# Layer 1's low weight parts made by an accumulating DMA instead of a subtraction on DVE

## The chip, the cores and the metric

The kernel runs on one core of one Trainium2 chip, as one program with one launch. The metric is the device time of an execution in microseconds (us). An execution that was recorded by the hardware profiler gives the rows that are read here; a profiled execution's span runs from its first to its last instruction.

## The reference, cut to what matters

A trunk of two layers over 512 positions with 1024 channels, in float32, then a final norm:

- Layer 0 is a hybrid of two recurrent mixers (an S5 state space and a Mamba-2 SSD), with an input projection, gates and an output projection.
- Layer 1 is multi-scale retention: RMSNorm, one input projection [q | k | v | gate] with 4 heads (256 wide for q and k, 512 wide for v), rotary on q and k, the decayed scores and their product with v, a norm per head, `silu(gate)` times the normed output, an output projection, and the residual add.

```python
p = (h @ w_in).astype(F32)                 # 1024 x 6144
...
y = jax.nn.silu(g) * o
return y.astype(w_out.dtype) @ w_out       # 2048 x 1024
```

The kernel computes its weight products with float32r matmuls. It writes each operand as a high part (the value as rounded to float32r) and a low part (what is left of it), and sums three products: high by high, high by low, low by high.

## The kernel before, in words

Activations stand transposed, channels on partitions and the 512 positions along the free axis; each 128-channel piece has a high tile and a low tile made once. Weights come from HBM as tiles of 128 x 8 x 128 numbers (512 KB). `ld_w` (L93) takes a raw buffer (tag `raw`, two of them), has SP start the load (L96) and calls `split_w` (L99), which takes a high buffer (tag `wh`, two) and a low buffer (tag `wl`, two) and issues two instructions: ACT copies raw into the float32r high tile, which rounds it (L105), and DVE subtracts the high tile from raw into the low tile (L106). `mm3` (L109) then runs 24 matmuls of 128x128 by 128x512 per tile, three for each of the 8 k: high weight by high activation (L113), high weight by low activation (L114), low weight by high activation (L115), all into one PSUM bank. So a tile's low part is first read by its third matmul.

Layer 1 takes 60 tiles through `ld_w`: for each head 4 for q and k (named `qk...`, by `proj`, L848) and 4 for v (`v...`, L882, with 4 PSUM banks at a time, L887 to L889), 16 for the gate (`g0` to `g15`, L943), 8 for the first half of the output projection (`out0` to `out7`, L960) and 4 for the second half's first columns (`on0` to `on3`, L993, L998 to L1000). The order in the program is qkv(0), qkv(1), gate(0), gate(1), out0 to out7, qkv(2), qkv(3), gate(2), gate(3), on. The second half's last columns (`om0` to `om3`, L1003 to L1011) load into the same `raw` buffers, but are split by `split` (L117), halves of 512 columns with ACT (L118) and DVE (L119), into buffers of their own. Everything else that PE does in layer 1 (scores and their products with v, L874; norms, L164 and L170; transposes, L971) goes between the tiles' matmuls.

POOL does little in layer 1: the rotary's sums (`rt`, L861), the sums of squares of a head's output (`os`, L930) and of the layer's input (`hs`, L840), and one product of the final norm (L1023).

No order is written by hand here. The builder (a tile framework) tracks which instruction reads and writes which buffer, plays the program through a model of the engines' times, and puts each engine's instructions in the order in which they become ready there, ties by rank: `rank_w` (L86) gives weight splits a rank ahead of all else after the setup, `rank_e` (L90) gives evictions the next. On the chip each engine then takes its instructions strictly in that order, each waiting on semaphores for what it needs. A buffer is taken again when the last reader of its former tile is done: `wh` after the last L114 of the tile two before, `wl` after its last L115, `raw` after its split.

Of the kernel before, what the change touches and what calls it, by code (L numbers as in the profile page):

```python
# [11 lines left out]
F32 = mybir.dt.float32  # L12
F32R = mybir.dt.float32r
I32 = mybir.dt.int32
AF = mybir.ActivationFunctionType
ALU = mybir.AluOpType

P = 128
SEQ = 512
D = 1024  # L20
KD = D // P
# [27 lines left out]
def trunk_kernel(ctx: ExitStack, tc: tile.TileContext, a: dict, out: bass.AP):  # L49
    nc = tc.nc  # L50
    vec, act, pool, pe, sp = nc.vector, nc.scalar, nc.gpsimd, nc.tensor, nc.sync

    cp = ctx.enter_context(tc.tile_pool(name="cp", bufs=1))
    wp = ctx.enter_context(tc.tile_pool(name="wp", bufs=2))
# [16 lines left out]
        return t  # L71

    wcount = [0]
    wdma = {}

    def after(name):
# [2 lines left out]
    @contextmanager  # L79
    def rank(v):  # L80
        old = tc.cur_priority
        tc.cur_priority = v
        yield
        tc.cur_priority = old

    def rank_w():  # L86
        wcount[0] += 1
        return rank(-2000000 + 20 * wcount[0])
# [4 lines left out]
    def ld_w(src, name, halves=1, ahead=0):  # L93
        raw = wp.tile([P, KD, P], F32, name=name + "w", tag="raw", bufs=2)
        with rank(tc.cur_priority - ahead):
            wdma[name] = sp.dma_start(raw, src).ins  # L96
        return split_w(raw, name, halves)

    def split_w(raw, name, halves=1):  # L99
        h = wp.tile([P, KD, P], F32R, name=name + "h", tag="wh", bufs=2)  # L100
        lo = wp.tile([P, KD, P], F32R, name=name + "l", tag="wl", bufs=2)
        n = KD // halves
        with rank_w():
            for k in range(0, KD, n):
                act.activation(h[:, k:k + n], raw[:, k:k + n], AF.Copy)  # L105
                vec.tensor_tensor(lo[:, k:k + n], raw[:, k:k + n], h[:, k:k + n].bitcast(F32), op=ALU.subtract)  # L106
        return h, lo
# [77 lines left out]
    def layer0():  # L185
        xh, xl, sq = [], [], []

        def proj(src, name, tag="acc", ahead=0):
            ps = acc(name) if tag == "acc" else aux(name, tag)
            mm3(ps, ld_w(src, name, ahead=ahead), xh, xl)  # L190
            return ps
# [268 lines left out]
        for m in range(8):  # L460
            ps = acc(f"gl{m}")
            mm3(ps, ld_w(a["w_glu"][m], f"gl{m}"), y5h, y5l)
            with rank_e():
                sg = t("p", f"sg{m}")
                act.activation(sg, ps, AF.Sigmoid, bias=chp[:, 3, m:m + 1])
                vec.tensor_tensor(sg, sg, za[m], op=ALU.mult)
                h, lo = t("x", f"yah{m}", F32R), t("x", f"yal{m}", F32R)
                split(sg, h, lo)
            yah.append(h), yal.append(lo)
        for m in range(KD):  # L470
            ps = acc(f"ob{m}")
            mm3(ps, ld_w(a["w_o0"][m, 1], f"ob{m}"), ybh, ybl)
            with rank_e():
                if m % 2 == 0:
                    xp = f(f"h{m}", [P, 2, SEQ])
                x = xp[:, m % 2]
                with after(f"ob{m}"):
                    sp.dma_start(x, a["xT"][m])
                vec.tensor_tensor(x, ps, x, op=ALU.add)  # L479
                hT.append(x)  # L480
# [546 lines left out]
                sp.dma_start(out[c * P:(c + 1) * P, i * 512:(i + 1) * 512], fin[c][i])  # L1027

    layer0()
    layer1()  # L1030


# [60 lines left out]
def _build(arrays):  # L1093
    import concourse.bacc as bacc

    nc = bacc.Bacc("TRN2", target_bir_lowering=False, num_devices=1)
    aps = {k: nc.dram_tensor(f"in_{k}_dram", v.shape, F32, kind="ExternalInput").ap() for k, v in arrays.items()}
    out = nc.dram_tensor("out_0_dram", (SEQ, D), F32, kind="ExternalOutput").ap()
    with tile.TileContext(nc, schedule_with_timeline_sim=True) as tc:
        trunk_kernel(tc, aps, out)  # L1100
    return nc
# [9 lines left out]
```

## Time and profile before

| what | value |
|---|---|
| time, three executions | 935.73, 935.9, 938.51 us; median 935.9 |
| profiled execution, span | 934.4 us (the page lists no other time of this execution) |
| PE (matmul) busy | 857.8 us, 92% of the span |
| DVE busy | 637.8 us, 68% |
| ACT busy | 350.3 us, 37% |
| POOL busy | 287.0 us, 31% |
| moved by DMA | 117.47 MB |

PE is TensorE's matmuls (PEld its weight loads, which overlap them), DVE is VectorE, ACT ScalarE, POOL GpSimd, SP the engine whose queue issues the DMAs. Shares of busy time are averages over stages with different limits: layer 0 fills the first 500 us or so, layer 1 the rest, and DVE's 68% is mostly layer 0's. In a timeline row the bracket says how long the engine was idle before the instruction and what ended that idle time.

### The profile page before, as it was taken

How to read it: one execution, taken by the hardware profiler on the slowest of the kernel's cores; microseconds unless marked ns; L12 is line 12 of the kernel's file. 1: busy time of each engine (PE TensorE's matmuls, PEld its weight loads, DVE VectorE, ACT ScalarE, POOL GpSimd, SP SyncE). 2: the span in 40 equal slices, each digit the busy share in tenths (PEclk: the TensorE clock that was granted, in tenths of full speed). 3: DMA queues.
4: the chain of work that ended last, by engine and by line, in shares of the span. 5: the costliest groups of instructions: out<-in, count | busy, mean ns of one | idle time of the engine just before them, and what ended most of it. 6: DMA issues, size and time to landing. Idle time of an engine off the chain costs nothing.

```text
span 934.4 us, 11848 instructions
## 1 busy us (share of the span) xinstructions
PE 857.8 (92%) x4408; PEld 691.0 (74%) x4408; DVE 637.8 (68%) x1086; ACT 350.3 (37%) x504; POOL 287.0 (31%) x217
## 2 busy tenths in 40 slices
PE   7995589788888988899999999999999999999996
PEld 5773467666666876677888888888888888888885
DVE  7999999999999468885344454744633644447455
ACT  5132124111235677564233235245421243254432
POOL 7039963576755223900013021201000303110020
PEclk9997789978899999899999999999999999999999
DMA  5376357545478876224423221221223221212322
GB/s 168 113 186 164 73 143 198 158 120 167 136 191 271 257 240 237 80 101 147 180 90 107 94 85 54 90 71 66 90 93 109 90 83 54 90 68 67 113 91 90
DMA packets 71609, 117.47 MB, mean 126 GB/s; under 512 B 27328, under 2 KB 37888, under 8 KB 71424
## 3 DMA queue, kind: packets, MB, share of 16 engines
q1 hardware_dynamic: 71552, 116.72, 40.4%
q8 instruction: 35, 0.57, 0.3%
q14 instruction: 22, 0.18, 0.1%
HBM read 101.71 MB, written 14.97 MB: 125 GB/s over the span
## 4 chain that ended last, share of the span: by engine, by line
PE 57%; DVE 1%; ACT 0%; issue 0%; ACTq 0%
PE g L113 3%; PE qk L115 3%; PE qk L114 3%; PE g L115 3%; PE g L114 3%; PE qk L113 3%; PE v L889 3%; PE v L887 3%; PE v L888 3%; PE ob L113 2%; PE oa L114 2%; PE oa L115 2%; PE oa L113 2%; PE ob L114 2%; PE ob L115 2%; PE out L115 1%
## 5 line engine op out<-in xcount | busy, mean ns | idle before, releaser
L861 POOL TENSOR_TENSOR rt<-rt,ru 128x512 f32<-128x512 f32 x16 | 27.2, 1721 | 137.6 <-DVE ru L860 137.6
L930 POOL TENSOR_TENSOR os<-os,os 128x512 f32<-128x512 f32 x12 | 15.5, 1291 | 143.3 <-ACT os L928 143.3
L840 POOL TENSOR_TENSOR hs<-hs,hs 128x512 f32<-128x512 f32 x7 | 12.6, 1805 | 105.0 <-ACT hs L838 105.0
L325 DVE SCALAR_TENSOR_TENSOR cva<-pad,cvw,cva 128x512 f32<-128x512 f32 x36 | 40.9, 1140 | 0.1
L860 DVE TENSOR_TENSOR ru<-qk,tab 128x512 f32<-128x512 f32 x16 | 10.9, 683 | 33.7 <-PE qk L115 33.7
L762 POOL TENSOR_TENSOR O<-ct,s5pws 128x512 f32<-128x512 f32 x16 | 22.8, 1427 | 32.4 <-DMA ct<-in_s5c_dram 20.6
L327 ACT ACTIVATE cva<-cva 128x512 f32<-128x512 f32 x12 | 7.6, 630 | 55.2 <-DVE cva L325 55.2
L323 ACT ACTIVATE cva<-pad,cvw 128x512 f32<-128x512 f32 x12 | 9.8, 813 | 49.2 <-DVE pad L321 49.2
L766 POOL TENSOR_TENSOR O<-O,ot 128x512 f32<-128x512 f32 x16 | 27.6, 1747 | 0.1
L762 POOL TENSOR_TENSOR ot<-ct,s5pws 128x512 f32<-128x512 f32 x16 | 26.6, 1661 | 0.6 <-DVE mg L746 0.6
L377 POOL TENSOR_TENSOR ssdb<-ssdb,cva 128x1024 f32<-128x1024 f32 x6 | 17.4, 2905 | 29.9 <-ACT ssdb L376 23.5
L1023 POOL TENSOR_TENSOR fin<-fin,fnw 128x512 f32<-128x512 f32 x4 | 6.0, 1525 | 61.5 <-ACT fq L987 61.5
L962 DVE TENSOR_TENSOR h<-h,out 128x512 f32<-128x512 f32 x8 | 5.5, 686 | 25.5 <-PE out L115 25.5
L479 DVE TENSOR_TENSOR h<-ob,h 128x512 f32<-128x512 f32 x8 | 5.5, 690 | 25.4 <-PE ob L115 25.4
L486 DVE TENSOR_TENSOR h<-h,oa 128x512 f32<-128x512 f32 x8 | 5.5, 688 | 21.9 <-PE oa L115 21.9
L366 DVE TENSOR_SCALAR ssdb<-ssdb,nacs 128x128 f32<-128x128 f32 x64 | 15.2, 303 | 6.8 <-DMA ssdb<-at_d 6.8
L712 POOL TENSOR_TENSOR tm<-al,b 128x512 f32<-128x512 f32 x6 | 10.4, 1750 | 29.2 <-DMA b<-in_s5bP_dram 22.8
L383 PE MATMUL y<-ssdb,xdt 128*64 128x128 f32 x128 | 13.8, 300 | 4.6 <-DVE ssdb L368 4.6
L371 POOL TENSOR_TENSOR xds<-xdt,dcd 128x512 f32<-128x512 f32 x6 | 7.6, 1270 | 32.1 <-DVE xdt L356 32.1
L491 POOL TENSOR_TENSOR s5rt<-rot,s5lv 128x512 f32<-128x512 f32 (+4 forms) x7 | 5.6, 803 | 38.1 <-DVE s5lv L647 35.8
L367 ACT ACTIVATE ssdb<-ssdb 128x1024 f32<-128x1024 f32 x8 | 8.5, 1057 | 23.1 <-DVE ssdb L366 23.1
L383 PEld LDWEIGHTS y<-ssdb,xdt 128*64 128x64 f32 x128 | 9.0, 145 | 9.9 <-DVE ssdb L368 5.3
(1784 smaller groups left out, 3177.2 us busy)
## 6 DMA issues: line engine op xcount, KB each, us to landing
al<-al_d SPq DMA_DIRECT2D x64, 64.0 KB, 3.5
b<-in_s5bP_dram SPq DMA_DIRECT2D x8, 512.0 KB, 4.2
o_d<-O SPq DMA_DIRECT2D x16, 256.0 KB, 2.7
T<-kd SPq DMA_DIRECT2D x64, 64.0 KB, 3.6
ssdb<-at_d SPq DMA_DIRECT2D x8, 512.0 KB, 4.9
Or<-o_d SPq DMA_DIRECT2D x16, 256.0 KB, 4.8
x<-in_xT_dram SPq DMA_DIRECT2D x8, 256.0 KB, 5.0
u_d<-us SPq DMA_DIRECT2D x8, 256.0 KB, 3.1
```

The costliest lines, as they stand in the source:

```text
L113: pe.matmul(ps, wh[:, k, :], xh[k], start=start and i == 0, stop=False)
L114: pe.matmul(ps, wh[:, k, :], xl[k], start=False, stop=False)
L115: pe.matmul(ps, wl[:, k, :], xh[k], start=False, stop=stop and i == len(ks) - 1)
L325: vec.scalar_tensor_tensor(g, pad[:, j:j + SEQ], cvw[:, m, j:j + 1], g, op0=ALU.mult, op1=ALU.add)
L377: pool.tensor_tensor(abc, abc, cT[gr][:, cs].unsqueeze(1).broadcast_to([P, 8, P]), op=ALU.mult)
L383: pe.matmul(o, xdt[:, i, :], dec[:, i, :], start=True, stop=c == 0)
L762: pool.tensor_tensor(x.rearrange("p (g k c) -> p g k c", g=4, c=16), ct[:, c, par, 4 * hf:4 * hf + 4].unsqueeze(2).broadcast_to(sh), pws[: ...
L766: pool.tensor_tensor(o, o, tm, op=ALU.add)
L861: pool.tensor_tensor(t1, t1, t2, op=op)
L887: pe.matmul(ps[c], hh[kk][:, cs], wh[:, i, :], start=kk == 0, stop=False)
L888: pe.matmul(ps[c], hh[kk][:, cs], wl[:, i, :], start=False, stop=False)
L889: pe.matmul(ps[c], hl[kk][:, cs], wh[:, i, :], start=False, stop=kk == KD - 1)
```

## The change

In layer 1 (a flag is set between the two layers) `ld_w` splits a tile with a new function. ACT makes the high part as before, then a second copy of raw with scale -1 into the low buffer, again as float32r, which is the negative of the high part. POOL then issues a DMA that adds raw to the low buffer, both in SBUF, so that it holds raw minus the high part. DVE has no part in it. Layer 0 and the `om` tiles keep the subtraction.

```diff
     wcount = [0]
+    by_dma = [False]
     wdma = {}
...
-        return split_w(raw, name, halves)
+        return split_d(raw, name) if by_dma[0] else split_w(raw, name, halves)
+
+    def split_d(raw, name):
+        h = wp.tile([P, KD, P], F32R, name=name + "h", tag="wh", bufs=2)
+        lo = wp.tile([P, KD, P], F32R, name=name + "l", tag="wl", bufs=2)
+        with rank_w():
+            act.activation(h, raw, AF.Copy)
+            act.activation(lo, raw, AF.Copy, scale=-1.0)
+            pool.dma_start(lo.bitcast(F32), raw, accum_op=ALU.add)
+        return h, lo
...
     layer0()
+    by_dma[0] = True
     layer1()
```

## Rows read from the trace of the kernel before

**Rows 1.** The page's busy time of each engine.

```profile
PE 857.8 (92%) x4408; PEld 691.0 (74%) x4408; DVE 637.8 (68%) x1086; ACT 350.3 (37%) x504; POOL 287.0 (31%) x217
```

**Rows 2.** By stretch: busy us (count) of PE, PEld, DVE, ACT, POOL; clock; DMA.

```profile
514.70:602.00 87.30, 87.30 (x407) 71.98 (x406) 47.28 (x83) 31.15 (x48) 18.75 (x12) 1.00 0.23 79
...
858.00:903.40 45.40, 45.40 (x216) 37.38 (x215) 22.85 (x30) 19.81 (x31) 0.00 (x0) 1.00 0.34 116
...
sum 419.70, PE 411.34 PEld 339.52 DVE 214.78 ACT 155.63 POOL 50.45; mean PE 58.76 PEld 48.50 DVE 30.68 ACT 22.23 POOL 7.21
```

**Rows 3.** Waits of PE, 500 to 935 us: total, times, longest.

```profile
PE out L115 <- DVE out2l L106: 0.2, 1, 0.2
```

**Rows 4.** Timeline of ACT: start us, duration us, line, operation, idle before.

```profile
684.25 1.06 ACT L105 ACTIVATE out2h<-out2w 128x1024 fp32r<-128x1024 f32 x1 [5.65 <-PE out L114]
...
702.60 1.06 ACT L105 ACTIVATE out6h<-out6w 128x1024 fp32r<-128x1024 f32 x1 [4.38 <-PE out L114]
...
893.29 1.04 ACT L105 ACTIVATE on3h<-on3w 128x1024 fp32r<-128x1024 f32 x1
...
904.98 0.62 ACT L118 ACTIVATE wh<-om3w 128x512 fp32r<-128x512 f32 x1
```

**Rows 5.** Timeline of DVE.

```profile
703.70 1.23 DVE L106 TENSOR_TENSOR out6l<-out6w,out6h 128x1024 fp32r<-128x1024 f32 x1 [0.18 <-ACT out6h L105]
...
894.37 1.23 DVE L106 TENSOR_TENSOR on3l<-on3w,on3h 128x1024 fp32r<-128x1024 f32 x1 [0.26 <-ACT on3h L105]
...
905.63 3.13 DVE L119 TENSOR_TENSOR wl<-om3w,wh 128x512 fp32r<-128x512 f32 x2
```

**Rows 6.** Instructions of line 113: duration ns min/median/max, first and last start us.

```profile
L113 PE MATMUL out<-yh,out6h x8: 389/389/389, 708.1 to 712.8; 128*128 128x512 f32 x8
...
L113 PE MATMUL out<-yh,out7h x8: 389/389/389, 713.5 to 718.3; 128*128 128x512 f32 x8
```

**Rows 7.** DMA issues: count, KB each, median us from issue to landing.

```profile
qk000w<-in_w_qk_dram SPq DMA_DIRECT2D x1, 512.0 KB, 3.3
...
on3w<-in_w_o1b_dram SPq DMA_DIRECT2D x1, 512.0 KB, 3.2
...
out_dram<-fin SPq DMA_DIRECT2D x8, 256.0 KB, 2.1
...
tab<-in_tab_dram SPq DMA_DIRECT2D x1, 1536.0 KB, 7.9
```

**Rows 8.** Timeline of POOL.

```profile
517.08 1.80 POOL L840 TENSOR_TENSOR hs<-hs,hs 128x512 f32<-128x512 f32 x1 [3.64 <-ACT hs L838]
...
576.24 1.29 POOL L930 TENSOR_TENSOR os<-os,os 128x512 f32<-128x512 f32 x1 [32.96 <-ACT os L928]
...
581.02 1.29 POOL L930 TENSOR_TENSOR os<-os,os 128x512 f32<-128x512 f32 x1 [1.67 <-ACT os L928]
583.90 3.52 POOL L861 TENSOR_TENSOR rt<-rt,ru 128x512 f32<-128x512 f32 x2 [1.59 <-DVE ru L860]
```

**Rows 9.** Timeline of SP's DMA queue: issue us, duration us.

```profile
895.62 0.33 SPq L1006 DMA_DIRECT2D om1w<-in_w_o1b_dram  x1
...
900.77 0.33 SPq L1006 DMA_DIRECT2D om3w<-in_w_o1b_dram  x1
```

**Rows 10.** Timeline of PE.

```profile
125.57 0.79 PE L115 MATMUL xbc<-xh,xbc1l 128*128 128x512 f32 x1 [2.97 <-DVE xbc1l L106]
...
340.53 0.40 PE L802 MATMUL Y<-Or,X 128*64 128x128 f32 x2 [1.98 <-DMA Or<-o_d]
...
907.96 0.40 PE L1020 MATMUL om<-wl,yh 128*128 128x512 f32 x1
```

**Rows 11.** By stretch, in layer 0: columns as in rows 2.

```profile
126.00:128.00 2.00, 2.00 (x6) 1.52 (x6) 2.00 (x3) 0.00 (x0) 1.92 (x2) 0.50 0.75 166
128.00:130.00 2.00, 2.00 (x9) 1.59 (x8) 2.00 (x2) 0.00 (x0) 1.92 (x3) 0.79 0.94 340
...
340.00:342.00 2.00, 1.15 (x14) 0.94 (x15) 1.23 (x1) 2.00 (x4) 0.74 (x2) 1.00 0.75 206
```

## The prediction

> **What bounds the kernel now.** I read the page's busy shares first. PE is busy for 92% of the span, DVE 68%, ACT 37%, POOL 31% [rows 1]. The change touches layer 1 alone, so next I read the engines by stretch. From 514.7 us to the end of the last full tile at 903.4 us PE never rests (87.30 us busy of 87.30 at its beginning, 45.40 of 45.40 at its end), at a granted clock of 1.00, the level of 2.4 GHz [rows 2]. The list of waits agrees: for a low part PE waited once in all of layer 1, 0.2 us [rows 3]. So layer 1 is bound by PE, and DVE's subtraction costs nothing there now. What matters is whether the new way still delivers a low part before PE wants it.
>
> One weight tile in detail, from layer 1's output projection. ACT's high copy of out6 starts at 702.60, when PE has done its last high-part matmul of out4 and so frees the buffer (two per tag), and takes 1.06 us [rows 4]. DVE subtracts from 703.70 for 1.23 us, done at 704.93 [rows 5]. PE begins out6 at 708.1 and out7 5.4 us later; its eight L113 steps of three matmuls stand 0.67 apart, so a matmul takes 0.22, and the third, the first that reads the low part, comes at 708.5 [rows 6]. **The cover** is 5.9 us from the start of the split to the first use, of which 2.3 are used and 3.6 are spare. In the other stages, with tiles of 5.6 us, it is 6.1.
>
> **The change, part by part.** It concerns 60 tiles (16 qk, 16 v, 16 g, 8 out, 4 on), one weight load of 512 KB each; the om tiles keep the old way.
>
> *Removed*: 60 DVE subtractions of 1.23 us, 74 us of DVE. They lie beside PE's work [rows 3, 5]: worth 0 to 0.2 us; I take 0.
>
> *Added on ACT*: a second 1.06 us copy per tile, 64 us. ACT is busy 156 of 420 us there [rows 2], so it fits, but it stands in series in the split: both copies are done 2.2 us after the start.
>
> *Added on POOL and the DMA engines*: an issue and a transfer per tile that reads 512 KB of raw and 512 KB of the destination and writes 512 KB. I call A the time from the end of the second copy to the landing. The trace has no transfer of this kind and none issued by POOL, so I bound it. Low end: a plain 512 KB load lands 3.2 to 3.3 us after issue (the first and the last of the 60) [rows 7], so A = 3.3; a 256 KB store already takes 2.1 [rows 7]. High end: all 1536 KB as the table's load, 7.9 us [rows 7], plus an issue as long as POOL's longest tensor operation here, 1.8 us [rows 8]: A = 9.7. Between: the two loads differ by 4.6 us for 1024 KB, so a second stream of 512 KB adds 2.3 to 3.3, which makes 5.6. SP's issue, 0.33 us [rows 9], is in that; an issue made by POOL's software I put at the middle between it and 1.8, so 0.7 more. **A = 6.4**: nearest to the load's row plus one more read, which is what the operation does.
>
> The Trainium skill speaks for less (DMA: Bandwidth & Descriptors, Anatomy of one DMA — SWDGE path): 2.0 us and the bytes at 436 GB/s, an estimate of 3.2 us for 512 KB. It also says (Collectives: The Full Stack, The bandwidth ceiling) that an add in the DMA engines reads two sources through one ring and so runs at half a copy's rate; with both, the estimate is 4.4. No row here shows either. The first would give some 940 us by the replay below, the second about 950.
>
> *What that does to PE.* A split lasts 2.2 + 6.4 = 8.6 us against 5.9 to 6.1: the first tile is 2.6 us late. The tile behind it has begun its split meanwhile and is then in time, because PE was held for 2.6 us; the one after that is late again. So each pair of back-to-back tiles loses 2.6 us, 78 us for 30 pairs. Against that: 388.7 us of PE less 60 tiles of 5.5 leaves 59 us of attention and norm matmuls, part of which falls between a split's start and its use. I replayed PE's matmuls in the trace's order and spacing, with each split started when its buffers come free and ready 8.6 us later. The waits by stretch: first head's qk and v 10.6, second head's 4.4, first gates 6.7, out0 to qk211 19.8 (out2 alone 6.1, because out0 and out1 are interleaved and free their buffer late: its copy waited until 684.25 already [rows 4]), third head's v 4.2, fourth head's qk and v 5.1, last gates 4.7, on 3.1. **Sum 58.6 us.** The same replay gives 4 us at A = 3.3, 7 at 3.85, 15 at 4.5, 36 at 5.5, 104 at 8 and 155 at 9.7.
>
> *Moved: the release of raw.* SP loads the next tile but one into raw when the subtraction has read it; now when the transfer has landed. For the 60 tiles that is covered: PE's own work on the tile, 5.4 us, hides the 3.3 us load. At the tail it is not. on3's split begins at 893.29, its subtraction ends at 895.60 and om1's load is issued at 895.62; om1's raw frees om3's load, issued at 900.77 [rows 4, 5, 9]. With on3's raw freed 8.6 us after the start instead of 2.3, om1 and om3 move 6.3 us back. om3's split begins at 904.98 and ends at 908.76 [rows 4, 5], and PE reads its first low part at 907.96 [rows 10]: of the 6.3 us some 2 are spare, and PE stands 4 us. **+4 us** (2 to 8). SP's queue holds little else there than loads that wait for the same buffers.
>
> *POOL's queue*: layer 1 has few entries (16 rotary sums, 12 square sums); POOL waits up to 33 us between them [rows 8]. The split has the highest rank after the setup, so I take 0; the price if an issue stands behind a sum is a rival.
>
> *The clock.* In layer 0, PE waited 2.97 us for xbc1's low part until 125.57 and then ran at half clock, 1.2 GHz, until about 129 (0.50, then 0.79) [rows 10, 11]: 1.7 us lost in addition. After a wait of 1.98 us, until 340.53, the clock stayed full [rows 10, 11]. Nine of the replayed waits reach 2 us or more; I let five of them cost 1.7: **+8 us**, between 0 and 30.
>
> *Sum*: 58.6 + 4 + 8 = 71. The profiled span is 934.4 us; the median of the runs, 935.9, lies 1.5 above it, and I keep that: 935.9 + 71 = **1007 us**.
>
> **The rivals.**
>
> *Hidden after all (the other side).* The transfer is on chip on both ends and lands like a load or sooner; A up to 3.85. Then the 3.6 us of spare cover hold, and the kernel gives 936 to 943; below A = 2.8 nothing is measurable. For it: loads of the same size land in 3.2 to 3.3 us [rows 7]. Against it: two reads instead of one and an issue by software. It decides at A of about 3. Chance 0.12, of it 0.03 that a new order of instructions makes it faster, 0.05 no change, 0.04 slightly slower. By the estimate of 3.2 us from the Trainium skill (DMA: Bandwidth & Descriptors, Anatomy of one DMA — SWDGE path) it would be this case.
>
> *A slow adder.* If adding halves or thirds the rate again, A is 8 or more, and PE waits for nearly every pair by 4 to 6 us. At 9.7: 155, 7 for the tail (9.6 later, 2 to 3 spare) and 30 for the clock (18 of the waits halve it) make 1128 us; at 8, about 1070. Nothing in the trace shows the adder's rate either way. Chance 0.20.
>
> *POOL's order.* Square sums of one head run from 576.24 to 582.31 with ACT waits between them, and pairs of rotary sums take 3.5 us [rows 8]. An issue put behind these is late by up to 6.1 us in each of 4 heads and 3.5 in each of 8 pairs: 4 x 6.1 + 8 x 3.5 = 52 us on top, 1059. Against it: the high rank. Chance 0.10.
>
> *The forecast itself*, A between 3.85 and 8: 943 to 1070 us. Chance 0.58.
>
> **How the numbers follow.** The likeliest case gives 1007. The range runs from 944 (A a little over the cover) to 1120 (A about 9.4 with the clock's share); outside lie the hidden case, 0.12, and the far end of the slow adder, some 0.08. A measurement here can tell about 0.3%, 2.8 us, from no change. Faster comes from the hidden case alone, 0.03; same 0.05; the rest is slower, 0.92.
>
> **What would show it.** In the profile after: PE's waits would name the low parts, released by a DMA instead of DVE, on about every second tile; in the out stage waits near 2.6 us; ACT's busy time up by some 64 us, DVE's down by 74; about 61 MB more on a queue of POOL's own, with a landing near 5.7 to 6.4 us; om1 and om3 loads later after on3; half-clock stretches in layer 1. The prediction is wrong if the landing is under 4 us (then the waits vanish), if PE waits at every tile (A over 8), if the waits stand behind POOL's sums, or if the builder, whose own model of the transfer sets the order, moves the attention work into the gaps.

## The result and the profile after

The changed kernel takes 966.92 us (median of 4 runs, 964.83 to 971.17) against 935.82 for the kernel before: ratio 1.0338, interval 1.0312 to 1.0364. It is slower by 31 us. I had forecast 1007 with a range of 944 to 1120: the sign is right and the range holds it, but the loss is less than half of the 71 us that I had summed. The profiled execution took 967.5 us, its span 965.6.

The page's busy time of each engine, and the first line of its chain that ended last:

```profile
PE 868.1 (90%) x4408; PEld 691.3 (72%) x4408; DVE 569.1 (59%) x1026; ACT 405.9 (42%) x564; POOL 333.5 (35%) x277
...
PE 49%; DVE 21%; DMA 16%; issue 7%; ACT 4%; SPq 2%; POOL 1%; ACTq 0%; DVEq 0%; POOLq 0%
```

Against [rows 1], DVE is down by 69 us, ACT up by 56, POOL by 46.5 (each issue is counted there). PE has 4408 matmuls as before; what is new is the DMA in the chain, of which the page of the kernel before names none. Layer 1 by stretch (columns as in [rows 2]; the last row is the om stage):

```profile
513.70:601.00 87.30, 83.71 (x385) 67.49 (x384) 29.73 (x66) 42.31 (x59) 24.56 (x24) 1.00 0.62 147
601.00:907.00 306.00, 292.14 (x1309) 234.27 (x1309) 95.99 (x176) 147.07 (x204) 61.11 (x62) 0.99 0.64 151
907.00:934.00 27.00, 23.63 (x104) 18.56 (x103) 4.12 (x6) 9.37 (x13) 2.58 (x3) 1.00 0.71 181
934.44:965.60 31.16, 22.96 (x121) 19.24 (x119) 19.35 (x63) 11.00 (x27) 6.18 (x4) 0.93 0.23 85
```

PE, which never rested there before [rows 2], now has gaps in every stretch. What it waits for (waits of PE: total, times, longest) answers to [rows 3], the largest first:

```profile
PE out L125 <- DMA out6l<-out6w: 1.9, 1, 1.9
PE g L125 <- DMA g3l<-g3w: 1.6, 1, 1.6
PE out L125 <- DMA out0l<-out0w: 1.6, 1, 1.6
PE v L898 <- DMA v00l<-v00w: 1.6, 1, 1.6
```

All are low parts, released by a DMA, and all are small: none reaches 2 us. The list has 29 low parts in layer 1 and 20.8 us, while layer 1, from PE's first qk to its first om matmul, takes 420.7 us against 388.5. The list understates the loss: matmuls start 0.23 us apart but each row lasts 0.39, so 0.16 of every wait counts as busy, and the first matmul behind a wait stands 0.11 longer before the next. I estimate 8 us for both together.

The rest is the clock. The granted clock averages 0.99 to 1.00 in the rows above, but it fell twice to 0.50, which is 1.2 GHz, for about 3.4 us each: as PE's wait of 1.6 us for g3's low part ended, and 0.7 us after its wait of 1.3 for qk311's:

```profile
654.00:657.00 3.00, 2.87 (x7) 2.30 (x8) 1.92 (x8) 0.63 (x1) 0.28 (x1) 0.50 0.75 130
818.00:821.00 3.00, 3.00 (x9) 2.32 (x8) 0.00 (x0) 0.00 (x0) 0.00 (x0) 0.50 1.02 161
```

Each costs about 1.7 us. The longer wait for out6 and waits of 1.6 for out0 and v00 had no such stretch behind them.

The chain of waits in the out stage shows how a wait comes about (start us, duration us, what):

```profile
700.01 0.50 PE out L125
...
705.20 0.92 issue
706.12 1.05 ACT out4l L105
707.17 0.29 issue
707.46 4.77 DMA out4l<-out4w
712.27 0.50 PE out L125
```

This is one turn of a low buffer, of which there are two. PE begins to read out2's low part at 700.01; at 706.12 ACT writes out4's negative into the same buffer, 1.05; after 0.29 POOL issues, and 4.77 later the sum is there. 12.26 us for two tiles, where PE's own work on two is 2 x 5.4 [rows 6]. The 0.92 that the chain calls issue, between PE's last reads and the negative, is ACT's high copy. PE's last two reads of out2, and ACT's timeline:

```profile
704.68 0.39 PE L124 MATMUL out<-yl,out2h 128*128 128x512 f32 x1
704.91 0.39 PE L125 MATMUL out<-yh,out2l 128*128 128x512 f32 x1
```

```profile
705.15 1.06 ACT L104 ACTIVATE out4h<-out4w 128x1024 fp32r<-128x1024 f32 x1 [4.24 <-PE out L124]
706.12 1.04 ACT L105 ACTIVATE out4l<-out4w 128x1024 fp32r<-128x1024 f32 x1
```

The high copy starts 0.08 us after PE's last read of its buffer ends (705.07). The low buffer is free at 705.30, but the negative stands behind the high copy in ACT's order and starts only when that is nearly done. Where ACT is idle it starts 0.04 to 0.16 us after such a read ends, so the high copy costs the turn about 0.7 us, by estimate. It stands first in 44 of the 60 tiles. The 16 with the negative first have 2 of the 29 waits, 1.0 us of the 20.8; but they lie where attention matmuls give a split more time, so this is no test of the order.

Two of the larger waits come from the order of instructions and not from this turn. For g3 ACT made a table load and one of the gate's activations between the high copy (645.30) and the negative (648.22). For qk311 POOL's issue stood behind two rotary sums, 2.0 us after the negative was done.

In the out stage the turn sets the pace; POOL's timeline shows the issues 6.2 us apart (24.65 us for four) instead of 5.4, a loss of about 0.7 at each tile:

```profile
701.21 0.86 POOL L106 DMA_DIRECT2D out3l<-out3w  x1 [5.13 <-ACT out3l L105]
...
725.86 0.86 POOL L106 DMA_DIRECT2D out7l<-out7w  x1 [5.29 <-ACT out7l L105]
```

The transfer itself, from the DMA view: the queues between 500 and 970 us (packets, MB, share of 16 engines' time), and then three of the 60 landings with the queues in the same stretch.

```profile
q0 software_dynamic: 8640, 31.46, 35.5%
q1 hardware_dynamic: 10656, 36.18, 23.9%
...
q0 software_dynamic: 144, 0.52, 61.7%
...
qk111l<-qk111w POOLq DMA_DIRECT2D x1, 512.0 KB, 4.5
...
q0 software_dynamic: 144, 0.52, 36.8%
q1 hardware_dynamic: 144, 0.52, 31.1%
...
on2l<-on2w POOLq DMA_DIRECT2D x1, 512.0 KB, 7.2
...
on3l<-on3w POOLq DMA_DIRECT2D x1, 512.0 KB, 7.3
```

The landings run from 4.5 to 7.3 us, median 5.1, mean 5.3. qk111l had the engines to itself: 4.5. Beside on2l a whole weight load of 0.52 MB moved: 7.2. All seven that were issued with no other data queue in their stretch, qk111l one of them, land in 4.5 to 4.7. A load beside it does not settle the landing alone: out5l had 0.47 MB of one beside it and landed in 4.7. What else makes a landing late was not followed up.

### The profile page after: what moved, and what is told of

Its sections match the earlier page's. It is cut to its first block, busy times and chain, and to the rows that moved or that the text cites. A ratio compares the mean times of both kernels' runs of the same rounds, so it can differ in the third digit from the quotient of the medians.

```text
span 965.6 us, 11980 instructions
## 1 busy us (share of the span) xinstructions
PE 868.1 (90%) x4408; PEld 691.3 (72%) x4408; DVE 569.1 (59%) x1026; ACT 405.9 (42%) x564; POOL 333.5 (35%) x277
## 3 DMA queue, kind: packets, MB, share of 16 engines
q0 software_dynamic: 8640, 31.46, 17.3%
## 4 chain that ended last, share of the span: by engine, by line
PE 49%; DVE 21%; DMA 16%; issue 7%; ACT 4%; SPq 2%; POOL 1%; ACTq 0%; DVEq 0%; POOLq 0%
PE v L898 3%; PE v L899 3%; PE v L897 3%; DVE cva L335 2%; PE g L125 2%; PE qk L125 2%; PE g L124 2%; PE g L123 2%; PE qk L123 2%; PE qk L124 2%; PE ob L123 2%; PE gl L124 2%; PE ob L124 1%; PE gl L125 1%; PE ob L125 1%
## 5 line engine op out<-in xcount | busy, mean ns | idle before, releaser
L871 POOL TENSOR_TENSOR rt<-rt,ru 128x512 f32<-128x512 f32 x16 | 22.3, 1402 | 26.7 <-DVE ru L870 26.7
L722 POOL TENSOR_TENSOR tm<-al,b 128x512 f32<-128x512 f32 x6 | 12.5, 2097 | 29.6 <-DVE gi L740 23.0
L129 DVE TENSOR_TENSOR rl<-rt,rh 128x512 fp32r<-128x512 f32 (+1 forms) x16 | 16.2, 1026 | 7.4 <-ACT rh L128 7.2
```

The lines of the kernel that those rows point to most:

```text
L871: pool.tensor_tensor(t1, t1, t2, op=op)
```

## The experiments

My theory after this: PE stands because an accumulate lands 5.1 us after its issue, longer than a turn of the two low buffers leaves room for. Rivals: the second copy on ACT, the issue by POOL's software, the traffic as such, the order of the copies.

### The second copy alone

```diff
-            pool.dma_start(lo.bitcast(F32), raw, accum_op=ALU.add)
+            vec.tensor_tensor(lo, raw, lo.bitcast(F32), op=ALU.add)
```

> Both ACT copies stay; DVE adds raw to the negative copy where the DMA did it. Theory (the time lies in the transfer): the split is two copies of 1.06 us and a DVE operation near 1.2, together 3.4 us after the start against a cover of 5.9, so PE waits for almost no low part: 934 to 938 us. Rival (the second copy in series on ACT, or ACT's extra 64 us, sets the time): most of the 31 us stay, 955 or more; a half-way value near 945 would say that ACT has a part in it.

Measured: 937.99, ratio 1.0025 (1.0009 to 1.0041). ACT is as busy as in the changed kernel (406.6 us), and 2 of the 31 us are there. The rest comes with the transfer.

### The same transfer without the addition, from POOL and from ACT

```diff
-            pool.dma_start(lo.bitcast(F32), raw, accum_op=ALU.add)
+            pool.dma_start(lo.bitcast(F32), raw)      # one kernel
+            act.dma_start(lo.bitcast(F32), raw)       # the other
```

> POOL issues a plain copy of raw onto the low buffer, with no accumulation; this leaves the addition out, so the low part is raw itself. Theory (the second read and the addition make the transfer long): it lands about 1.2 us sooner, near 3.8 us from the issue in place of 5.1, and PE's waits fall to a few us: 936 to 942 us. Rival (the issue by POOL's software is what makes it long): the landing stays at 4.8 to 5.2 us, and the time at 960 to 970.

> The same plain copy with no addition (left out, as in the run beside it), issued on ACT's queue in place of POOL's. Theory (the second read is the cost, not who issues): lands within 0.5 us of POOL's plain copy, and the time is within 4 us of that run. Rival (POOL's software issue is over 1 us of the landing): lands near the loads' 3.3 us, and the time is 934 to 938 whatever POOL's plain copy gives.

Measured: 937.16, ratio 1.0016 (1.0003 to 1.0029), from POOL, and 938.09, 1.0019 (1.0002 to 1.0036), from ACT. In the kernel with POOL's copy every engine has the changed kernel's instructions in the changed kernel's order (but for two neighbours on DVE in layer 0), so the 29.8 us between the two are the accumulation alone, with what it does to landing and issue. Its DMA view (the queue between 500 and 970 us, a landing) and POOL's timeline:

```profile
q0 software_dynamic: 8640, 31.46, 16.8%
...
out6l<-out6w POOLq DMA_DIRECT2D x1, 512.0 KB, 2.9
```

```profile
705.14 0.53 POOL L106 DMA_DIRECT2D out6l<-out6w  x1 [4.91 <-ACT out6l L105]
710.58 0.53 POOL L106 DMA_DIRECT2D out7l<-out7w  x1 [4.91 <-ACT out7l L105]
```

The same packets and bytes take 16.8% of the engines' time instead of 35.5, about half, and the median landing is 2.9 instead of 5.1. POOL's issue takes 0.53 instead of 0.86 us. With 2.9 the issues are 5.44 us apart, PE's own pace. From ACT's hardware queue the same copy lands no sooner (one of them, and that queue's row between 700 and 715 us):

```profile
q10 hardware_dynamic: 432, 1.57, 26.3%
...
out5l<-out5w ACTq DMA_DIRECT2D x1, 512.0 KB, 2.9
```

So the software issue, for which I had put 0.7 us into A, costs the landing nothing; the second read and the addition, which no run here separates, cost it 2.2. The Trainium skill (Collectives: The Full Stack, The bandwidth ceiling) says of the reduce step of a collective that it reads two sources through one ring and so runs at half the rate of a copy. The two shares here, 35.5 and 16.8%, agree with that.

### The negative first

```diff
-            act.activation(h, raw, AF.Copy)
             act.activation(lo, raw, AF.Copy, scale=-1.0)
             pool.dma_start(lo.bitcast(F32), raw, accum_op=ALU.add)
+            act.activation(h, raw, AF.Copy)
```

> The rounded negative and the DMA's issue come before the high copy, so that the transfer starts 1.06 us earlier after raw and the buffers are there. Theory (PE waits for what the split is longer than the cover, at each tile): a replay of PE's matmuls in the changed kernel's order, with its own landings 1.06 us earlier, gives 11 us of waits in place of 31: about 945 us (940 to 952). Rival (the transfer is slow because of what else moves on the DMA engines at that time, and so lands when that is over): no change, 963 to 970.

Measured: 962.73, ratio 1.0277 (1.0253 to 1.0302). This experiment tested nothing. The builder put the same instructions in the same order as for the changed kernel (but for two neighbours on DVE in layer 0), whatever the order of the lines: in the out stage the high copy, whose buffer comes free first, still runs first. What the run gives is a second measurement of the changed kernel, 4.2 us under the first; below, differences of that size between kernels with the accumulate are not read. What the order is worth stays untested, and it is a rival for a part of the loss: in the turn above the low buffer is free at 705.30 and the negative starts at 706.12, so with two buffers a negative ahead of the high copy would, by estimate, save about 0.7 of the 1.4 us that the turn is too long. The high copy has the time: it is done at 706.21 and first read at 711.33.

### A third low buffer

```diff
-        lo = wp.tile([P, KD, P], F32R, name=name + "l", tag="wl", bufs=2)
+        lo = wp.tile([P, KD, P], F32R, name=name + "l", tag="wl", bufs=3)
-BUFS = {'x': 16, 'v': 17, 'm': 20, 's': 4, 'p': 5, 'f': 8}
+BUFS = {'x': 16, 'v': 17, 'm': 20, 's': 3, 'p': 5, 'f': 8}
```

The first line stands in both split functions, so layer 0 has the third buffer as well. One kernel so, one with the negative first besides, and one with p cut to 4 in place of s.

> A third low buffer (one buffer of layer 0's small tag s is given up for the room), copies in the changed kernel's order, high first. Theory (PE stands for the way from its last read of a low buffer to the landing of the tile that comes next into it, 0.9 + 1.05 + 0.3 + 5.1 us; and ACT makes the negative behind the high copy, which waits for the high buffer that PE frees at almost the same moment): the third buffer alone is no use, since the high copy ahead of it in ACT's order holds the negative back: 960 to 968 us. Rival (the low buffer's return alone is the bound): 934 to 942.

> The third low buffer, and the negative and the DMA's issue ahead of the high copy. Theory (as in the run beside it): now neither buffer holds the negative back, the transfer starts up to a tile (5.4 us) earlier, and 5.1 us from issue to landing are hidden: 934 to 942 us. Rival (the accumulate's load on the DMA engines, 17 per cent of all sixteen, or its landing however early it starts, costs the time): 955 or more.

> The third low buffer again, with the room taken from tag p (5 buffers to 4) in place of s. Theory (the return of the low buffer is the bound, and a third one hides it): layer 1's waits for low parts stay under 3 us and its length up to the last projection within 3 us of before; with what the smaller p costs in layer 0 and 4 us at the tail, 937 to 946 us. Rival (the gain of the earlier runs came from the order of instructions that the smaller s led to): PE waits as in the changed kernel, 955 or more.

Measured: 947.29 (1.0120, 1.0100 to 1.0140), 947.45 (1.0127, 1.0096 to 1.0157; again the same instruction order as the first) and 942.55 (1.0086, 1.0062 to 1.0110). The first two fell between their theories and their rivals, and the first tested neither of its own: with a third buffer free the builder itself puts the negative ahead, in all 60 tiles, as ACT's timeline of the first shows. L105 now stands before L104, and the negative waits for the load alone, so buffer and order changed together:

```profile
694.84 1.06 ACT L105 ACTIVATE out4l<-out4w 128x1024 fp32r<-128x1024 f32 x1 [1.55 <-DMA out4w<-in_w_o1a_dram]
697.10 1.06 ACT L104 ACTIVATE out4h<-out4w 128x1024 fp32r<-128x1024 f32 x1 [1.20 <-PE out L124]
```

And PE's waits in the third kernel's layer 1 before the on tiles are these two, where the changed kernel's list, the on tiles included, names 29 low parts:

```profile
PE v L898 <- DMA v21l<-v21w: 1.3, 1, 1.3
PE out L125 <- DMA out7l<-out7w: 0.7, 1, 0.7
```

The accumulates land as late as before (median 5.1), but PE's first qk matmul to its first on matmul takes 367.7 us there (518.71 to 886.41) and 369.1 in the first, against 394.3 in the changed kernel (513.70 to 907.97) and 366.7 in the kernel before (514.72 to 881.41). So the third buffer, with the earlier negative that it allows, gives back 25 to 27 of layer 1's 27.6 us up to there, at the same traffic: the traffic as such is not the cause. How much of that is the buffer and how much the order no run separates. The third kernel met its theory. Of what these kernels still lose, about half or more sits in layer 0: layer 1 begins at 520.2 in the first and 518.7 in the third. I took that for the price of the smaller tag, and ran the control.

> The kernel before, with the tag s cut from 4 buffers to 3 and nothing else: the control to the two runs with a third low buffer, which gave 947 and in which layer 1 began at 520.2 us against 514.7 before. Theory (half of the 11 us that those runs lost is the price of the buffer given up in layer 0, and not of the accumulate): 940 to 943 us, layer 1 beginning 5 to 6 us later. Rival (layer 0 is as before, and the 11 us belong to the new way): 935 to 937.

The edit is the second pair of lines alone, on the kernel before. Measured: 935.19, ratio 0.9995 (0.9984 to 1.0006), layer 1 beginning at 511.3. The smaller s costs nothing, and my theory for it fell. So the 5.5 us that the first loses in layer 0 (against 514.7; 8.9 against the control) came with the third buffer in the tag that both layers share; which instructions lose them was not followed up. For the 4.0 us of the kernel with the smaller p no control was run.

### Halves

```diff
+            for k in (0, 4):
+                act.activation(h[:, k:k + 4], raw[:, k:k + 4], AF.Copy)
+                act.activation(lo[:, k:k + 4], raw[:, k:k + 4], AF.Copy, scale=-1.0)
+                pool.dma_start(lo[:, k:k + 4].bitcast(F32), raw[:, k:k + 4], accum_op=ALU.add)
```

> Two low buffers, but high copy, negative and accumulate are made in two halves of four k's each. Theory (the bytes make the landing long): a half of 256 KB lands 3.2 to 3.8 us after its issue instead of 5.1, and its copy takes 0.5 instead of 1.05, so the first read comes 2 us sooner after the buffer's release, where 1.4 per pair of tiles are missing in the out stage; the second half is needed 2.7 us later: 934 to 944 us. Rival (most of the 5.1 us is the same for any size, and two issues on POOL with 0.9 us each come on top): the halves land after 4.5 us or more, and the time stays at 950 or more.

Measured: 960.66, ratio 1.0249 (1.0227 to 1.0271), 2 us under the lower of the two measurements of the changed kernel: a miss, and the rival's time. The DMA view of tile out4l (landings of its two halves), then the chain of waits:

```profile
DMA to landing us min/median/max: 3.3/3.8/4.3
```

```profile
711.52 3.95 DMA out6w<-in_w_o1a_dram
...
716.72 1.05 ACT out6l L106 x2
...
718.21 0.43 POOL out6l L107
...
718.75 5.81 DMA out6l<-out6w
...
724.70 4.19 DMA qk200w<-in_w_qk_dram
```

Out4's first half lands in 3.3 us, but the second is issued behind it and shares the engines with it and with the next load: 4.3 for out4, 5.8 for out6. Over the 60 tiles the first halves land in 3.2 to 6.9 us, median 4.3, so the 3.2 to 3.8 that I expected held for only 19 of them. raw is free only when the second has landed, and the next load waits for that: from out6w's load at 711.52 to the load that takes the same raw buffer, 724.70, is 13.2 us for two tiles. In this stretch the wait moved from the low buffer to raw.

### Half by DVE, half by DMA

```diff
+            act.activation(h, raw, AF.Copy)
+            vec.tensor_tensor(lo[:, 0:4], raw[:, 0:4], h[:, 0:4].bitcast(F32), op=ALU.subtract)
+            act.activation(lo[:, 4:8], raw[:, 4:8], AF.Copy, scale=-1.0)
+            pool.dma_start(lo[:, 4:8].bitcast(F32), raw[:, 4:8], accum_op=ALU.add)
```

> k 0 to 3 of each low part by DVE's subtraction as before, k 4 to 7 by ACT's negative and the accumulate; two low buffers. Theory (what counts is the landing against PE's first read of those bytes): a 256 KB accumulate lands 3.4 us after its issue, as the first halves of the earlier run did, and its bytes are first read 2.7 us later than the tile's first; that is 4.4 us sooner against the need than in the changed kernel, more than the 1.4 us per pair that were missing: 935 to 940 us. Rival (the accumulate's traffic as such, or the waits of ACT and POOL in a row, costs the time): half of the 31 us stay, 948 or more.

Measured: 937.87, ratio 1.0025 (1.0013 to 1.0036). DVE is still relieved of 28 us (609.4 against 637.8 [rows 1]), and the one wait for a low part in PE's list of layer 1 is this; beside it a landing and the queue between 500 and 970 us:

```profile
PE v L899 <- DMA v20l<-v20w: 0.8, 1, 0.8
```

```profile
q0 software_dynamic: 8640, 15.73, 19.8%
...
out4l<-out4w POOLq DMA_DIRECT2D x1, 256.0 KB, 3.3
```

The median landing is 3.3 us here (the expectation's "as the first halves of the earlier run did" is wrong, their median was 4.3). So 256 KB accumulates at 60 tiles cost no more than the second copy on ACT; that fits the theory that what decides is when the bytes land against PE's first read of them. The traffic of the accumulates is halved as well, but the third low buffer has shown that traffic is not the cause.

### Where DVE is the bound

```diff
+            by_dma[0] = o[0] in "xz"      # in layer 0's loop over its order
+        by_dma[0] = False
-    by_dma[0] = True                      # ahead of layer 1
```

> The new way (negative first) for the x and z tiles of layer 0 alone, where DVE is busy 198.4 of 200 us between 100 and 300 us; layer 1 with the subtraction as before. Theory (the new way pays where DVE is the bound): 28 subtractions of 1.23 us, 34 us, leave DVE, of which some half shortens the kernel: 912 to 930 us. Rival (POOL, busy 125 of these 200 us, issues late, or the longer split makes PE late): 940 to 965.

Measured: 985.00, ratio 1.0522 (1.0499 to 1.0546), worse than the rival's bound. Layer 1 is as before (366.7 us from its first qk to its first on matmul), but begins at 564.8. The waits of POOL before 514 us, and the stretch from 100 to 300 us with the columns of [rows 2]:

```profile
POOL z8l L105 <- ACT z8l L104: 12.3, 1, 12.3
POOL z0l L105 <- ACT z0l L104: 11.8, 1, 11.8
```

```profile
100.00:300.00 200.00, 139.26 (x764) 105.40 (x764) 159.42 (x158) 50.83 (x63) 119.32 (x94) 0.82 0.69 168
```

POOL takes its instructions in the builder's order, and the issue stands for up to 12 us for ACT's negative while the recurrences' work for POOL queues behind it. DVE's busy time fell to 159 us of 200 there as hoped, but PE's fell as well, from 160.4 us in the kernel before to 139.3, and the granted clock from 0.89 to 0.82: the work that bound this stretch had moved to waits. That POOL's queue is the cause is argued and not shown; how the 50 us divide between it, the later low parts and the clock was not taken apart.

## Why the prediction was right and wrong

**What bounds it, and the sign: right.** Layer 1 is bound by PE, the DVE time that it frees was worth nothing (the plain copy, which frees DVE too, is 1 us slower than before, not faster), and the loss is PE waiting for low parts that a DMA releases. The mechanism, a split longer than its cover, is the one that the runs show; the sizes failed.

**A, the landing: the term that failed most.** I forecast 6.4 us from the end of the second copy to the landing. (The parts add up to 6.3.) Measured: 0.29 to the issue and 5.1 median, 5.4. Of my parts, the base of 3.3 (a load from DRAM [rows 7]) is 2.9 for a copy within the chip; the second read, 2.3 from the table's row, is 2.2 with the addition; of the software issue's 0.7 the landing shows nothing, and the 0.29 from the copy to POOL's issue (0.03 to ACT's own) is all there is. The price of 1 us is large because the waits rise steeply once the cover is used: the prediction's own replay gives 58.6 us at 6.4, 36 at 5.5, and, run again, 33.5 at 5.4. That is 25 of the 40 us by which I was too high. It also fits the plain copy, 2.2 us sooner, which costs 1 us: the replay has 4 at 3.3. The two rules of the Trainium skill that I had weighed and not taken gave an estimate of 4.4 us for the accumulate together (DMA: Bandwidth & Descriptors, Anatomy of one DMA — SWDGE path; Collectives: The Full Stack, The bandwidth ceiling). The trace agrees where nothing moves beside it (4.5 to 4.7); over all tiles it has 5.1 in the median and up to 7.3.

**One landing for all tiles.** With the 60 measured landings instead of 5.4 for each, the replay in the order of before gives 45: the late ones, up to 7.3, add more than the early ones save.

**The order of PE's work: a term put at nothing.** I kept the order of before, though I named its change as a sign of being wrong. The builder moved other matmuls ahead of the first low read of some tiles (between v01's first matmul and its first low one stand 18 instead of 6, attention's for the most part; for v30 27 instead of none, most of them qk311's). The replay in the order after, with the measured landings, gives 31.3; layer 1 up to the om stage is 32 us longer. That the order is worth 14 is the replay's estimate; no run changed the order alone. That this and the spread of the landings nearly cancel is luck.

**The split itself: right in 44 tiles.** I had both copies in series behind the release of the high buffer, 2.2 us. In the out stage they stand so, 705.15 to 707.16 for out4, 2.0 us, and with the landing the split lasts 7.1 us instead of 8.6, against a cover of 5.9. A pair of tiles there loses 1.4 us, where I had 2.6. It loses about 0.7 at each tile instead of all at each second one. Waits at every tile were to be a sign of A over 8; they came at 5.4.

**The tail: 0 instead of 4.** om1's and om3's loads move back, as I said:

```profile
930.21 0.33 SPq L1016 DMA_DIRECT2D om1w<-in_w_o1b_dram  x1
...
935.43 0.33 SPq L1016 DMA_DIRECT2D om3w<-in_w_o1b_dram  x1
```

om3's load now comes 1.0 us after om's first matmul (934.44), where it came 2.4 ahead of it before, but the om stage, from its first matmul to its last, takes 23.2 us against 23.3. The builder put some reads of low parts later there. The on stage ahead of it, which I priced at 3.1, lost 4.7.

**The clock: 3.4 instead of 8.** I had nine waits of 2 us or more and let five of them cost 1.7. None reached 2, yet two waits, of 1.6 and 1.3, were followed by stretches at half clock. So the price of a stretch was right, and the place was not.

**The sum.** Against 71: 25 less for A, 11.5 more for the spread, 14 less for the order, 4 less for the tail, 4.6 less for the clock. That leaves 35 by these estimates, with 31 measured. With A alone put right it would have been 46.

**The rivals.** The hidden case decides where I put it: a landing of 2.9 is hidden, 5.1 is not. The slow adder fell, with a landing of 5.1 against 8. POOL's order came up once in layer 1 at a price, for qk311 after the sums of a head:

```profile
810.03 2.54 POOL L871 TENSOR_TENSOR rt<-rt,ru 128x512 f32<-128x512 f32 x2
812.52 0.84 POOL L106 DMA_DIRECT2D qk311l<-qk311w  x1
```

The issue is 2.0 us late, PE waits 1.3 and then runs at half clock: about 3 us and not 52. In the run with the new way in layer 0 it was the issues that stood in POOL's way. Of the signs, the 61 MB on POOL's queue were 31.46: its view has the same bytes for the accumulate as for the plain copy.

## What to carry to other kernels

When work moves from an engine to a longer path through a DMA, price the whole turn of the buffer (last read, copy, issue, landing, first read) against the number of buffers times the consumer's own pace. Here each turn, two tiles long, loses what it takes beyond that (12.3 against 10.9 us), and nothing is lost below it. Count in the turn what the refilling engine does first, as the high copy here. One more buffer, with the refill started earlier, or giving the slow path only the bytes that are read last, hides the same transfer. An accumulating DMA occupied the engines twice as long as a copy of the same bytes (35.5 against 16.8%). Look at what the builder made of an edit before its time is read: two of these edits changed no order at all.

## What the runs showed that I had not expected

- An accumulate of 512 KB within the chip lands in 4.5 to 4.7 us when alone and in 4.5 to 7.3 beside a weight load; I had one figure for all.
- A plain copy of 512 KB lands 2.9 us after its issue both from POOL's software queue and from ACT's hardware queue.
- The accumulate also makes POOL's issue longer, 0.86 us instead of 0.53.
- What a chain calls issue can be work: in the 0.92 us between PE's last reads of out2 and ACT's negative, ACT makes the high copy.
- PE's clock halved after waits of 1.3 and 1.6 us and not after one of 1.9.
